# The first packed tile of a two-layer decoder kernel, loaded in two transfers, with one product of zeros fewer ahead of it

## The chip, the cores and the metric

The kernel runs on one core of a Trainium2 chip. The metric is the device time of one execution in microseconds (us); a run is one execution, and the figure for a kernel is the median of its runs. The engines are named as in the profile: PE is the matrix engine (PEld its weight loads), DVE the vector engine, ACT the scalar engine, POOL the general-purpose engine, and SP the engine that issues most of the data transfers (DMAs).

## The reference, cut to what matters

A stack of two layers works on x, 256 tokens of 2048 features, in float32. The first layer is a Mamba-2 mixer, the second a sliding-window attention with a sink per head; each is followed by `layernorm(alpha * x + mixer(x))`.

```python
def reference(x, ...):
    x = layernorm(ALPHA * x + mamba2_mixer(x, a_w_in, ..., a_w_out))
    k, v = shared_kv(x, kv_w, kv_b, cos, sin)
    x = layernorm(ALPHA * x + swa_mixer(x, k, v, cos, sin, b_w_in, ..., b_w_out))
    return x

def mamba2_mixer(x, w_in, ...):
    zxbcdt = x @ w_in                  # z | x,B,C | dt
    dt = softplus(zxbcdt[..., -64:] + dt_bias)     # 64 heads: the step sizes
    ...
```

Only the very first product matters here, `x @ w_in`: its contraction runs over the 2048 features, that is 16 pieces (k = 0 to 15) of 128.

## The kernel before

**Precision.** TensorE is used in a reduced float32 format (fp32r). Every operand v is split into a high part h (a copy on ACT, L158 and L192) and a low part l = v - h (a subtraction on DVE, L161 and L193), and each product is three matmuls, h·h, h·l and l·h (`mac`, L238). The step sizes dt are the exception: they are multiplied in plain float32 (L369).

**Weights.** Weights come as *units* of 128x2048 floats. A unit is loaded in two halves of 512 KB (`load_half`, L149) and split half by half (`split_half`, L158 and L161). Units are loaded two ahead of the one in use (`AHEAD`), in the order of the list `srcs`.

**The start.** The first three units (`NF = 3`, three column blocks of w_in of 128 columns each) do not come as units. The host packs them with x into `first` (L1239): for every k a packed tile of 128 rows by `FW` = 704 floats, which holds 256 columns of x, 128 of each of the three blocks, and the 64 step-size columns at the end. `load_first` (L172) issues the 16 packed tiles one after another on SP's queue (L186), into buffers that are borrowed from other uses (`FIRST`, L33: some lie in the tile that the profile calls xr). For each packed tile it then splits four pieces in this order: x, block 0, block 1, block 2 (ACT at L192, DVE at L193).

`first_products` (L341) writes the order of TensorE's work by hand, with `keep_in_program_order`. First come `FILL[0]` = 6 matmuls of zeros (`fill`, L355), whose result nobody reads; the zeros are set by DVE at L344. Then `_order` (L35) runs over k: at k = 0 the step-size products of packed tile 0 (L369, two of 64x128), then for every k the three blocks' products, three matmuls each (L238, 128x256). Ahead of k = 2 stand `FILL[1]` = 3 more matmuls of zeros. The step-size products of packed tiles 1 to 3 stand ahead of k = 3, those of 4 to 6 ahead of k = 6 and those of 7 to 15 ahead of k = 13. After the 16 k follow the fourth unit and all others, through `block` (L674) and `narrow` (L335), in an order that the kernel plans by block.

**What sets the order.** TensorE's order is the written one. ACT and DVE are ordered by a scheduler that works from estimated times, with a few instructions pinned. SP issues its DMAs in program order. DMAs issued by SP and ACT take eight semaphores in turn, so that a DMA waits until the one eight places before it has landed.

Of the kernel before, what the change touches and what calls it, by code (L numbers as in the profile page):

```python
# [17 lines left out]
P = 128  # L18
S = 256
D = 2048  # L20
KT = D // P
# [3 lines left out]
NHD = 64  # L25
# [6 lines left out]
NF = 3  # L32
FIRST = [("wr", 1)] * 4 + [("yz", 1)] + [("e", 2)] * 2 + [("xr", 5)] + [("rb", 1)] * 2  # L33

def _order():  # L35
    steps = {0: (0, 1), 3: (1, 4), 6: (4, 7), 13: (7, 16)}
    o = []
    for k in range(KT):
        if k in steps:
            o.append((0, *steps[k]))  # L40
        if k == 2:
            o.append(None)
        o += [(i + 1, k, k + 1) for i in range(NF)]
    return o


FILL = [6, 3]

AGAIN = 5
FW = 256 + NF * 128 + 64  # L50

XK_AT = [15, 16, 17, 18]
ZPRI = 200
# [29 lines left out]
def trunk(ctx: ExitStack, tc: tile.TileContext, A: dict, out: bass.AP, dbg=None):  # L83
    nc = tc.nc
# [16 lines left out]
    def nm(s):  # L101
        uid[0] += 1
        return f"{s}_{uid[0]}"

    def mm_tile():
        return mm_ps.tile([P, 512], F32, tag="mm", name=nm("mm"), bufs=4)

    def ax_tile():
        return ax_ps.tile([P, 512], F32, tag="ax", name=nm("ax"), bufs=4)
# [28 lines left out]
    def new_unit(places):  # L138
        u = Unit()
        u.parts = []  # L140
        for tag, n, pl in (("wh", NH, places[0]), ("wl", NL, places[1])):
            t = wp.tile([P, 2112], F32R, tag=tag, name=nm(tag), bufs=n)
            u.parts.append([(t[:, o : o + (k1 - k0) * P], k0, k1) for o, k0, k1 in pl])
        u.h, u.l = u.parts[0][0][0], u.parts[1][0][0]
        return u
# [26 lines left out]
    def load_first():  # L172

        us = [new_unit([WHOLE, WHOLE]) for _ in range(NF)]
        raws = []
        for tag, n in FIRST:
            if tag == "xr":
                buf = xr_t
            elif tag == "wr":
                buf = wp.tile([P, 1024], F32, tag="wr", name=nm("first"), bufs=NR)  # L180
            else:
                w, bufs = {"rb": (1024, 2), "e": (1536, 2), "yz": (1024, 1)}[tag]
                buf = ap.tile([P, w], F32, tag=tag, name=nm("first"), bufs=bufs)
            raws += [buf[:, i * FW : i * FW + FW] for i in range(n)]
        for k, raw in enumerate(raws):
            nc.sync.dma_start(raw, A["first"][:, k, :])  # L186
            parts = [(xH(k, k + 1)[:, 0, :], xL(k, k + 1)[:, 0, :], raw[:, :S])]
            for i, u in enumerate(us):
                ks = slice(k * P, k * P + P)
                parts.append((u.h[:, ks], u.l[:, ks], raw[:, S + i * P : S + i * P + P]))  # L190
            for dh, dl, v in parts:
                nc.scalar.activation(dh, v, AF.Copy)  # L192
                nc.vector.tensor_tensor(dl, v, dh.bitcast(F32), ALU.subtract)  # L193
        return us, raws
# [36 lines left out]
    def next_unit():  # L231
        load_next(min(used[0] + 1 + AHEAD, len(srcs)) - len(units))
        used[0] += 1
        return units[used[0] - 1]
# [100 lines left out]
    def narrow(ps, u, k0, k1, pin=False, again=False):  # L335
        for k in range(k0, k1):
            ks = slice(k * P, (k + 1) * P)
            h, l = [x.again if again and k == 0 else x(k, k + 1)[:, 0, :] for x in (xH, xL)]
            mac(ps[:, :S], u.h[:, ks], u.l[:, ks], h, l, k == 0, k == KT - 1, pin)

    def first_products():  # L341

        zero = ap.tile([P, S], F32, tag="zz", name="zero", bufs=4)
        nc.vector.memset(zero[:], 0.0)  # L344
        zero = zero[:].bitcast(BF16)
        us, raws = load_first()
        units.extend(us)
        nc.sync.dma_start(pc[:], A["pc"])
        pss = [mm_tile() for _ in range(NF + 1)]
        ps = ax_tile()  # L350

        def fill(n):

            for _ in range(n):
                tc.keep_in_program_order(nc.tensor.matmul(ps[:], zero[:, :P], zero, start=True, stop=True))  # L355

        fill(FILL[0])
        for what in _order():
            if what is None:
                fill(FILL[1])  # L360
                continue
            i, k0, k1 = what
            if i:
                narrow(pss[i], us[i - 1], k0, k1, True)
                continue
            for k in range(k0, k1):
                for h in range(2):
                    tc.keep_in_program_order(
                        nc.tensor.matmul(  # L369
                            pss[0][64 * h : 64 * h + 64, :P], raws[k][:, S + NF * P :], raws[k][:, h * P : (h + 1) * P],  # L370
                            start=k == 0, stop=k == KT - 1,
                        )
                    )
        return pss
# [349 lines left out]
    def out_units(g, nbs):  # L724
        for nb in nbs:
            u = next_unit()
            for h in range(2):
                out_unit(*gs[g].y, h, u, nb, False, gs[g].rms)

    first_ps = first_products()  # L730
    dt_first, dt_second = make_dt(first_ps[0])
    load_next(1, True)
# [407 lines left out]
    for what, j in B_ORDER[:-1]:  # L1140
# [5 lines left out]
        else:  # L1146
            for nb in range(4):
                u = next_unit()
# [59 lines left out]
def _layout(inputs):  # L1208
    import numpy as np

    f = {k: np.asarray(v) for k, v in inputs.items()}
    c = np.ascontiguousarray
    a = {}
    x = f["x"][0]
    a["xt"] = c(x.T.reshape(KT, P, S).transpose(1, 0, 2))
    a["xk"] = c(x.reshape(2, P, D).transpose(1, 0, 2))

    def wstat(w):
        k, n = w.shape
        return c(w.reshape(k // P, P, n // P, P).transpose(2, 1, 0, 3).reshape(n // P, P, k))  # L1220

    def xstat(w, per, n):
        k, m = w.shape
        return c(
            w.reshape(k // (per * P), per, P, m // n, n).transpose(3, 0, 2, 1, 4).reshape(-1, P, per * n)
        )

    w = f["a_w_in"][0]
    o_xs, o_b, o_c, o_dt = DI, 2 * DI, 2 * DI + 1024, 2 * DI + 2048
    order = []  # L1230
    for g in range(NG):
        blk = [o_b + g * P, o_c + g * P]
        blk += [o_xs + g * 512 + i * P for i in range(4)]
        blk += [g * 512 + i * P for i in range(4)]
        order += [blk[k] for k in (BLOCKS0 if g == 0 else BLOCKS)]
    cols = np.concatenate([np.arange(s, s + P) for s in order])
    a["wa"] = wstat(w[:, cols])
    wdt = w[:, o_dt:].reshape(KT, P, NHD).transpose(1, 0, 2)
    a["first"] = np.concatenate([a.pop("xt")] + [a["wa"][i].reshape(P, KT, P) for i in range(NF)] + [wdt], 2)  # L1239
    conv = np.concatenate([f["a_conv_w"][0], f["a_conv_b"]], 0)  # L1240
    corder = []
    for g in range(NG):
        corder += [o_b - DI + g * P, o_c - DI + g * P] + [g * 512 + i * P for i in range(4)]
    cv = np.stack([conv[:, s : s + P] for s in corder], 0).transpose(2, 0, 1).reshape(P, 240)
    dsk = np.repeat(f["a_d"][0], 64).reshape(32, P).T
    nw = f["a_norm_w"][0].reshape(32, P).T
    two = lambda v: np.concatenate([v, v])[:, None]
    a["pc"] = c(np.concatenate([cv, dsk, nw, two(f["a_dt_bias"][0]), two(f["a_log"][0])], 1))
    wo = f["a_w_out"][0]
    a["wo"] = xstat(wo, 4, 512).reshape(4, NG, P, 2048).transpose(1, 0, 2, 3).reshape(32, P, 2048)  # L1250
    a["lng"], a["lnb"] = f["ln_g"], f["ln_b"]
    a["gbc"] = c(np.stack([f[k][0].reshape(KT, P).T for k in ("ln_g", "ln_b")], 1))
    a["wkv"] = xstat(f["kv_w"], 4, 512)
    a["kvb"] = f["kv_b"]
    wi = f["b_w_in"][0]
    a["wq"] = xstat(wi[:, :D], 4, 512)
    a["wg"] = wstat(wi[:, D:])
    a["qb"] = f["b_q_bias"][0]
    a["snk"] = f["b_sinks"][0].reshape(4, 4, 2).transpose(0, 2, 1).reshape(32)
    wb = f["b_w_out"][0]  # L1260
    a["wb"] = xstat(wb, 4, 512).reshape(4, 4, P, 2048).transpose(1, 0, 2, 3).reshape(16, P, 2048)
    a["pos"] = c(f["positions"][0].reshape(2, P).T)
    inv = (np.float64(500000.0) ** (-np.arange(0, 16, 2) / 16.0)).astype(np.float32)
    a["inv"] = np.tile(inv[None], (P, 1))
    i = np.arange(P)
    cc = np.zeros((P, 896), np.float32)
    cc[:, 0:128] = np.eye(P)
    cc[:, 128:256] = 1.0
    tri = (i[None, :] >= i[:, None]).astype(np.float32)
    cc[:, 256:384] = tri  # L1270
    cc[:, 384:512] = 1.0
    cc[:, 512:640] = tri
    cc[:, 640:768] = 1.0 - tri
    cc[:, 768:896] = np.where(i[None, :] <= i[:, None], 0.0, NEG)
    a["cc"] = cc
    return {k: c(v) for k, v in a.items()}
# [20 lines left out]
```

## Time and profile before

| | |
|---|---|
| three runs | 1001.87, 1002.36 and 1002.36 us; median 1002.36 |
| the profiled execution: own time | 1002.55 us |
| its span, first to last instruction | 1000.4 us |
| DVE / ACT / POOL busy, of the span | 77% / 57% / 10% |
| DMA | 198.81 MB, on average 199 GB/s |

In the profile's rows the first number is the start in us after the span's start, the second the duration, then engine, source line, operation, output<-inputs, shapes and count. A bracket at the end tells how long the engine was idle before the row and what ended that. "L238" is a line of the kernel before; after the change, lines behind L50 lie two or three further down. Packed tiles appear as `first` or, where the borrowed buffer is that one, as `xr`; `wh` and `wl` are the high and low parts of a unit, `xH` and `xL` those of x.

### The profile page before, as it was taken

To read this page: it belongs to the slowest core of one execution; us is meant where nothing else is said; L and a number is where in the kernel's file an instruction comes from. 1 tells how busy PE (TensorE), PEld (TensorE's weight loads), DVE (VectorE), ACT (ScalarE), POOL (GpSimd) and SP (SyncE) were. 2 spreads that over 40 slices of the span, in tenths; PEclk is the share of its full clock that TensorE was granted. 3 is DMA by queue.
4 is the path that set the end of the run, shared out by engine and by line. 5 is a ranking of instruction groups with operands and counts; after the bars stand their busy time and mean duration, and the time that the engine had idled before them with its cause. 6 is when DMAs were issued, how large, how long until landed. Compare 5 with 4: busy or idle time off the path is not lost.

```text
span 1000.4 us, 17835 instructions
## 1 busy us (share of the span) xinstructions
PE 993.4 (99%) x7036; PEld 899.6 (90%) x7036; DVE 774.6 (77%) x1189; ACT 566.1 (57%) x987; POOL 103.6 (10%) x128
## 2 busy tenths in 40 slices
PE   9999999999999999999999999999999999999997
PEld 8999989999999998999999999888988878878975
DVE  7888897867886886786786787898678775775686
ACT  7595856547746645664654764565545544544632
POOL 0001203004003003000300300303000000000002
PEclk9999999999999999999999999999999999999999
DMA  9798586565575666666656556457764546446422
GB/s 364 249 289 286 169 275 209 174 228 177 181 242 182 223 197 191 212 194 209 206 170 228 159 181 223 164 164 240 240 192 137 193 147 200 156 148 195 166 103 84
DMA packets 58963, 198.81 MB, mean 199 GB/s; under 512 B 6560, under 2 KB 10816, under 8 KB 58624
## 3 DMA queue, kind: packets, MB, share of 16 engines
q1 hardware_dynamic: 55792, 188.20, 57.3%
q0 software_dynamic: 2336, 8.69, 2.8%
q8 instruction: 55, 0.90, 0.4%
q10 hardware_dynamic: 752, 0.79, 0.2%
q14 instruction: 28, 0.23, 0.1%
HBM read 195.43 MB, written 2.23 MB: 198 GB/s over the span
## 4 chain that ended last, share of the span: by engine, by line
PE 95%; DVE 3%; ACT 1%; issue 1%; ACTq 0%; DVEq 0%
PE mm L238 52%; PE mm L945 10%; PE mm L305 8%; PE mm L306 8%; PE mm L307 8%; PE ax L610 2%; PE ax L1057 1%; PE ax L1115 1%; PE ax L586 1%; PE ax L1097 1%; DVE wl L161 1%; PE mm L369 0%; PE ax L569 0%; PE ax L1020 0%; DVE t L1196 0%
## 5 line engine op out<-in xcount | busy, mean ns | idle before, releaser
L161 DVE TENSOR_TENSOR wl<-wr,wh 128x1024 fp32r<-128x1024 f32 (+2 forms) x338 | 393.6, 1185 | 109.1 <-ACT wh L158 107.4
L158 ACT ACTIVATE wh<-wr 128x1024 fp32r<-128x1024 f32 (+2 forms) x338 | 332.7, 1011 | 205.9 <-issue 84.4
L238 PE MATMUL mm<-xH,wh 128*128 128x256 f32 x1280 | 356.1, 278 | 0.0
L238 PE MATMUL mm<-xL,wh 128*128 128x256 f32 x1280 | 354.4, 277 | 0.0
L238 PE MATMUL mm<-xH,wl 128*128 128x256 f32 x1280 | 354.3, 277 | 0.0
L238 PEld LDWEIGHTS mm<-xH,wh 128*128 128x128 f32 x1280 | 240.8, 188 | 2.1 <-ACT wh L192 0.7
L238 PEld LDWEIGHTS mm<-xL,wh 128*128 128x128 f32 x1280 | 240.8, 188 | 1.0
L238 PEld LDWEIGHTS mm<-xH,wl 128*128 128x128 f32 x1280 | 241.0, 188 | 0.0
L305 PE MATMUL mm<-wh,yH 128*128 128x512 f32 x256 | 101.4, 396 | 0.0
L306 PE MATMUL mm<-wh,yL 128*128 128x512 f32 x256 | 99.8, 390 | 0.0
L307 PE MATMUL mm<-wl,yH 128*128 128x512 f32 x256 | 99.7, 389 | 0.0
L626 POOL TENSOR_TENSOR yz<-yz,z 128x256 f32<-128x256 f32 x32 | 32.7, 1032 | 472.7 <-DVE yz L621 472.7
L238 PE MATMUL mm<-x1H,wh 128*128 128x256 f32 x256 | 71.7, 280 | 0.0
L473 DVE SCALAR_TENSOR_TENSOR cv<-mm,pc,cv 128x255 f32<-128x255 f32 x144 | 68.8, 478 | 3.3 <-ACT cv L471 1.9
L238 PE MATMUL mm<-x1L,wh 128*128 128x256 f32 x256 | 70.8, 277 | 0.0
L238 PE MATMUL mm<-x1H,wl 128*128 128x256 f32 x256 | 70.8, 276 | 0.0
L945 PE MATMUL mm<-wh,x1H 128*128 128x512 f32 x160 | 62.9, 393 | 0.0
L945 PE MATMUL mm<-wl,x1H 128*128 128x512 f32 x160 | 62.4, 390 | 0.1
L945 PE MATMUL mm<-wh,x1L 128*128 128x512 f32 x160 | 62.0, 390 | 0.0
L305 PEld LDWEIGHTS mm<-wh,yH 128*128 128x128 f32 x256 | 48.1, 188 | 10.3 <-DVE z L562 1.0
L307 PEld LDWEIGHTS mm<-wl,yH 128*128 128x128 f32 x256 | 48.1, 188 | 10.2
L312 DVE SCALAR_TENSOR_TENSOR xr<-mm,r,xr 128x512 f32<-128x512 f32 x64 | 47.2, 746 | 12.0 <-PE mm L307 7.6
(208 smaller groups left out, 1351.3 us busy)
## 6 DMA issues: line engine op xcount, KB each, us to landing
wr<-in_wa SPq DMA_DIRECT2D x154, 512.0 KB, 5.0
wr<-in_wo SPq DMA_DIRECT2D x64, 512.0 KB, 4.4
wr<-in_wq SPq DMA_DIRECT2D x32, 512.0 KB, 4.6
wr<-in_wg SPq DMA_DIRECT2D x32, 512.0 KB, 4.7
wr<-in_wb SPq DMA_DIRECT2D x32, 512.0 KB, 4.4
rb<-rscr SPq DMA_DIRECT2D x11, 512.0 KB, 4.3
wr<-in_wkv SPq DMA_DIRECT2D x8, 512.0 KB, 5.2
first<-in_first SPq DMA_DIRECT2D x11, 352.0 KB, 6.1
```

What stands on the lines that cost most here:

```text
L158: m = nc.scalar.activation(h[:, sl], v, AF.Copy)
L161: m = nc.vector.tensor_tensor(l[:, sl], v, h[:, sl].bitcast(F32), ALU.subtract)
L238: m = nc.tensor.matmul(ps, a, b, start=first and i == 0, stop=last and i == 2)
L305: pinned(nc.tensor.matmul(ps, aH[:, k, hs], u.h[:, ks], start=k == 0, stop=False), pin)
L306: pinned(nc.tensor.matmul(ps, aL[:, k, hs], u.h[:, ks], start=False, stop=False), pin)
L307: pinned(nc.tensor.matmul(ps, aH[:, k, hs], u.l[:, ks], start=False, stop=k == 3), pin)
L312: nc.vector.scalar_tensor_tensor(v, ps, rms[:, h : h + 1], v, ALU.mult, ALU.add)
L473: nc.vector.scalar_tensor_tensor(a[:, sft:], ps[:, : S - sft], w(3 - sft), a[:, sft:], ALU.mult, ALU.add)
L586: nc.tensor.transpose(ps[:, o : o + P], st.xs[i][:, c * P : (c + 1) * P], ident)
L610: nc.tensor.matmul(ps[64 * r : 64 * r + 64, cols], xd[:, c, r, :], e[:, 256:] if c else e[:, :256], start=c == 0, stop=c == 1,)
L626: nc.gpsimd.tensor_tensor(v, v, st.z[i][:], ALU.mult)
L945: m = nc.tensor.matmul(ps[:], (x1H, x1L, x1H)[i][:, kk, hs], (u.h, u.h, u.l)[i][:, ks], start=(kk, i) == (0, 0), stop=kk == KT - 1 and i == 2,
```

## The change

The packed tile keeps its 704 floats, but the 64 step-size columns now stand behind x and in front of the blocks. Packed tile 0 is loaded in two DMAs, the first of columns 0 to 447 (x, step sizes, block 0), the second of columns 448 to 703 (blocks 1 and 2). The other 15 tiles are loaded whole, as before. `FILL[0]` goes from 6 to 5.

```diff
-FILL = [6, 3]
+FILL = [5, 3]
...
-FW = 256 + NF * 128 + 64
+
+FW = 256 + 64 + NF * 128
+FCUT = 256 + 64 + 128
...
         for k, raw in enumerate(raws):
-            nc.sync.dma_start(raw, A["first"][:, k, :])
+            for c0, c1 in ((0, FCUT), (FCUT, FW)) if k == 0 else ((0, FW),):
+                nc.sync.dma_start(raw[:, c0:c1], A["first"][:, k, c0:c1])
             parts = [(xH(k, k + 1)[:, 0, :], xL(k, k + 1)[:, 0, :], raw[:, :S])]
             for i, u in enumerate(us):
                 ks = slice(k * P, k * P + P)
-                parts.append((u.h[:, ks], u.l[:, ks], raw[:, S + i * P : S + i * P + P]))
+                parts.append((u.h[:, ks], u.l[:, ks], raw[:, S + NHD + i * P : S + NHD + i * P + P]))
...
-                            pss[0][64 * h : 64 * h + 64, :P], raws[k][:, S + NF * P :], raws[k][:, h * P : (h + 1) * P],
+                            pss[0][64 * h : 64 * h + 64, :P], raws[k][:, S : S + NHD], raws[k][:, h * P : (h + 1) * P],
...
-    a["first"] = np.concatenate([a.pop("xt")] + [a["wa"][i].reshape(P, KT, P) for i in range(NF)] + [wdt], 2)
+    a["first"] = np.concatenate([a.pop("xt"), wdt] + [a["wa"][i].reshape(P, KT, P) for i in range(NF)], 2)
```

In the built program TensorE's order is otherwise the same, SP's has one DMA more, and POOL's is unchanged. The scheduler of ACT and DVE puts some instructions in another order: on ACT the evictions of the first three blocks (`in_z`, L561) now stand together, where before the first half of the fifth unit was split between them, and some ten instructions of ACT and DVE change places in the rest of the first group of blocks, before the second unit of the second group.

## The prediction

> **What bounds the kernel now.** I read the page's first lines, then TensorE's waits, then the start of the chain that ended last.
>
> ```profile
> span 1000.4 us, 17835 instructions
> PE 993.4 (99%) x7036; PEld 899.6 (90%) x7036; DVE 774.6 (77%) x1189; ACT 566.1 (57%) x987; POOL 103.6 (10%) x128
> ```
> ```profile
> PE ax L355 <- DVE zero L344: 1.2, 1, 1.2
> PE ax L1182 <- ACT dg L1171: 0.7, 1, 0.7
> ```
> ```profile
> 0.86 0.28 DVE zero L344
> 1.14 0.05 issue
> 1.19 2.74 PE ax L355 x6
> 3.93 0.63 PE mm L369 x4
> 4.56 3.25 PE mm L238 x18
> 7.81 0.66 PE ax L355 x3
> 8.47 1.06 PE mm L238 x9
> ```
>
> TensorE is busy for 993.4 of 1000.4 us, and the waits view lists two waits in the whole run: 1.2 us at the start, until the zeros are written, and 0.7 us in the tail. So there is no wait in between that this change could remove. A change at the start is worth just what it moves TensorE's whole stream forward, and it costs something only if it makes a wait where there is none. The reader is to see in the chain that TensorE goes from six products of zeros straight to the step-size products at 3.93 and the real ones at 4.56. What the change can win lies between 1.19 and 4.56, and one product of zeros is the whole of it.
>
> The rows of those first microseconds:
>
> ```profile
> 2.45 0.15 PEld L355 LDWEIGHTS <-zero 128*128 128x128 bf16 x1 [0.28 <-issue]
> 2.87 0.15 PEld L355 LDWEIGHTS <-zero 128*128 128x128 bf16 x1 [0.28 <-issue]
> ...
> 3.80 0.42 ACT L192 ACTIVATE xH<-first 128x256 fp32r<-128x256 f32 x1 [1.78 <-DMA first<-in_first]
> 3.86 0.30 PEld L369 LDWEIGHTS mm<-first 128*64 128x64 f32 x4 [0.84 <-DMA first<-in_first]
> ...
> 4.49 0.29 PEld L238 LDWEIGHTS mm<-xH,wh 128*128 128x128 f32 x1 [0.33 <-ACT wh L192]
> ```
>
> Zeros follow each other at 0.42 to 0.43 us (2.45 to 2.87). Packed tile 0 releases ACT at 3.80, just as the sixth ends. Two paths meet at the first real product: the zeros' end and the step-size products (3.93 + 0.63 = 4.56), and ACT's start plus 0.69 us for x and block 0 (3.80 to 4.49). Both must move.
>
> **The change, part by part.**
>
> *One product of zeros fewer.* TensorE is free at 3.93 - 0.43 = 3.50. Nothing else hangs on those zeros. This alone would gain nothing, since the data comes at 3.80; it would leave 0.3 us idle.
>
> *A shorter first transfer.* The first piece is 448 of 704 columns, 229 of 360 KB (128 rows of 1792 and 2816 bytes). The trace shows no transfer of this size at an empty queue; this is what it has:
>
> ```profile
> L186 SPq DMA_DIRECT2D first<-in_first x1: 384/384/384, 0.7 to 0.7; - x1
> ...
> DMA to landing us min/median/max: 3.0/3.0/3.0
> ```
> ```profile
> 1.00:2.00 1.00, 0.81 (x2) 0.28 (x3) 0.13 (x1) 1.00 (x1) 0.00 (x0) 1.00 0.28 34
> 2.00:3.00 1.00, 1.00 (x4) 0.43 (x3) 0.00 (x0) 0.01 (x1) 0.00 (x0) 1.00 0.86 276
> 3.00:4.00 1.00, 1.00 (x5) 0.16 (x5) 0.00 (x0) 0.20 (x1) 0.00 (x0) 1.00 1.06 411
> ```
> ```profile
> inv<-in_inv POOLq DMA_DIRECT2D x1, 4.0 KB, 1.9
> ```
>
> The last numbers of the window rows are GB/s: 34 KB have moved by 2.00, 310 by 3.00, and at 411 KB per us the 360 KB of tile 0 are through at 3.12. It lands at 0.74 + 3.0 = 3.74, so 0.62 lie between the last byte and the landing. The first 229 KB are through at 2.00 + 195/276 = 2.71, and land at 3.33: 0.41 us earlier. From the other side, 4 KB take 1.9 us and 360 KB 3.0 us; a straight line through the two gives 0.40 for 131 KB less. Bounds: nothing, if the landing of a first transfer is set by something other than its bytes; and at the other end 0.43, since TensorE isn't free before 3.50. I take 0.41, to which both rows lead.
>
> [...]
>
> *From 0.41 us of start to time at the end.* TensorE is slow here.
>
> ```profile
> 5.75 0.41 PE L238 MATMUL mm<-xH,wl 128*128 128x256 f32 x1
> ...
> 6.18 0.41 PE L238 MATMUL mm<-xL,wh 128*128 128x256 f32 x1
> ...
> 6.39 0.37 PE L238 MATMUL mm<-xH,wl 128*128 128x256 f32 x1
> ...
> 6.60 0.28 PE L238 MATMUL mm<-xH,wh 128*128 128x256 f32 x1
> ...
> 6.72 0.28 PE L238 MATMUL mm<-xL,wh 128*128 128x256 f32 x1
> ```
> ```profile
> 152.20 27.23 PE mm L238 x240
> ```
>
> The granted clock stands at 1.00 in every window row above, but the starts tell of two paces: 0.213 us a product up to 6.39 (three from 5.75) and 0.113 later (27.23/240). The step lies near 6.5 us, 5.3 us after the first product of zeros at 1.19. The zeros still start at 1.19, so I leave the step where it is. TensorE then does 0.41/0.213 = 1.9 products more before the step, and each saves what it would have cost after it: 1.9 x 0.113 = 0.22 us. Half of the gain is lost because it is won at half pace. If the step moved forward with the products, it would be the whole 0.41.
>
> [...]
>
> *The second piece (blocks 1 and 2), a new wait.* ACT's split of block 1 now waits for it, and so does DVE's; behind it in both queues stand block 2 and then packed tile 1, and TensorE's fourth product waits for ACT. ACT comes to it at 3.39 + 0.69 - 0.23 = 3.85 or later. The whole of tile 0 landed at 3.74; the second piece is issued at 0.74 + 0.42, while the engines still work on the first, so it lands about there. Cost: nothing. If it came 0.4 later, block 1's parts would be there at about 4.45, and its first product is due three cold products after 4.15, at 4.8.
>
> *One more DMA on SP.* Its 0.42 us push the issue of tiles 1 to 6 back; tile 7 must now wait for the first piece, which has long landed, and from tile 9 on each waits for the same tile as before. No POOL transfer stands near. How late could tiles 1 and 2 become?
>
> ```profile
> 5.53 0.69 DVE L193 TENSOR_TENSOR wl<-first,wh 128x128 fp32r<-128x128 f32 x3
> ...
> 5.94 0.42 ACT L192 ACTIVATE xH<-first 128x256 fp32r<-128x256 f32 x1 [0.22 <-DMA first<-in_first]
> ...
> 6.73 0.69 DVE L193 TENSOR_TENSOR wl<-first,wh 128x128 fp32r<-128x128 f32 x3
> ...
> 8.12 0.47 PE L238 MATMUL mm<-xH,wh 128*128 128x256 f32 x1
> ```
>
> Tile 1's low parts are done from 5.76 to 6.22; 0.42 later that is 6.18 for the first, which the third product of k = 1 needs at about 6.6. Tile 2's are done by 7.42, 0.70 ahead of the 8.12 at which TensorE comes to k = 2. Take 0.42 of lateness and 0.22 of earlier need away, and 0.06 stays for the last part, which is not needed before the ninth product. So the cost is nothing even at the bound, and the engines' backlog (the DMA share is 0.86 and more from 2.00 on) should hide most of the 0.42 anyway. From there ACT and DVE need under 1 us a tile and TensorE 1.05 and more, so the margin grows.
>
> *Reordered evictions on ACT and DVE.* The order of the two programs differs there.
>
> ```profile
> 26.62 0.38 ACT L561 ACTIVATE z<-mm 128x256 f32<-128x256 f32 x1 [1.48 <-PE mm L238]
> 26.90 1.05 ACT L158 ACTIVATE wh<-wr 128x1024 fp32r<-128x1024 f32 x1
> 27.85 0.65 ACT L561 ACTIVATE z<-mm 128x256 f32<-128x256 f32 x2
> ...
> 28.93 2.35 DVE L161 TENSOR_TENSOR wl<-wr,wh 128x1024 fp32r<-128x1024 f32 x2
> ...
> 66.57 1.22 DVE L161 TENSOR_TENSOR wl<-wr,wh 128x1024 fp32r<-128x1024 f32 x1
> ```
> ```profile
> 23.99 19.69 PE mm L238 x171
> ...
> 61.62 16.35 PE mm L238 x144
> ```
>
> The half unit that stood at 26.90 moves behind the two evictions, by at most 0.65 us. Its unit is the second after the packed ones: TensorE's 171 products from 23.99 begin it after 27 + 48, at 23.99 + 75 x 0.115 = 32.6, while DVE has its low parts at 31.3. 1.3 us of cover against 0.65. Later, one unit's low parts that were ready at 67.8 are due after 96 of the 144 products from 61.62, at 72.5: 4.7 us of cover against moves of one or two instructions of 1.2 to 1.8 us. Cost: nothing.
>
> Sum: -0.22 us. Against the profiled execution's own time 1002.55 that gives 1002.33; the median of the runs lies 0.19 lower, at 1002.36, so the forecast is 1002.14, say 1002.1. A measurement of this kernel tells about 0.2%, 2 us, from no change; this is a tenth of that.
>
> **The rivals.**
>
> *The landing doesn't move* (or only by a tenth). For it: the first transfer takes 3.0 us and 4 KB take 1.9, so most is not bytes. Then TensorE idles from 3.50 to about 3.86 and starts its work where it did: 1002.4, no change. The change does not do what it says.
>
> *The gap sets the pace back: slower.* If the data comes after 3.50, TensorE stands still up to 0.36 us, where the six zeros ran into the data. If standing still makes the count to the fast pace begin anew, the step comes 5.3 us after 3.86, at 9.2 instead of 6.5: 2.7 us more at the slow pace, each of which loses 1 - 0.113/0.213 = 0.47, so +1.27 us: 1003.6. It decides from the point where the first piece lands after 3.50. Against it: 0.36 idle in 5.3 us is 7%. No row here shows how long a stop it takes. [...]
>
> *A unit comes late after the reordering.* A wait of more than 2 us at one of the moved splits would be needed to be seen: 1004.5 and more. Against it stand the covers of 1.3 and 4.7 us.
>
> **How the numbers follow.** The forecast, a gain of 0.1 to 0.43, has 0.60. The landing that does not move has 0.15. The pace set back has 0.12. A late unit or several small losses together over 2 us: 0.10. A gain of more than 2 us, for which I see no place, since TensorE waits 1.9 us in all: 0.03. Faster 0.03, within 0.2% 0.87, slower 0.10. The forecast's own range is 1001.4 (the lowest run, 1001.87, less 0.43) to 1002.6. To leave out no more than 2 in 10 the range takes in the landing that doesn't move and the pace set back: 1001.4 to 1003.6.
>
> **What would show it.** Right: in the chain five zeros end at about 3.50, ACT's first split starts at about 3.4, the first product stands at about 4.15, the step in the pace stays near 6.5, and the first three units end about 0.2 us earlier. Wrong: a bracket of idle time before L369 that names the DMA, a step in the pace later than 7, a wait of ACT at block 1, or any third row in TensorE's waits.

## The result, and the profile after

| | before | after |
|---|---|---|
| median of 21 runs each, in turn on one chip | 1002.12 us (1001.77 to 1003.17) | 1003.15 us (1002.5 to 1006.93) |
| ratio after/before, 95% interval | | 1.0013 [1.0007, 1.0019] |
| profiled execution: own time, span | 1002.55, 1000.4 us | 1004.89, 1002.8 us |

The change made the kernel slower by about 1 us, where 0.22 us of gain was forecast. The profiled execution of after is one of its slower ones (1004.89 against a median of 1003.15); it shows the loss enlarged. The comparisons leave out one run of the experiment merged_fill6 (mean granted clock 0.557, 1671.66 us) and one of before in the same set (0.85, 1101.81 us).

TensorE's waits in after, each row in total us, times, longest:

```profile
PE mm L241 <- ACT wh L195: 1.6, 1, 1.6
PE ax L358 <- DVE zero L347: 1.2, 1, 1.2
PE ax L1185 <- ACT dg L1174: 0.7, 1, 0.7
```

The two waits of before are still there, and the first row is new: TensorE stands 1.6 us for a high part that ACT makes. The start of the chain that ended last (start, duration, what) says what ACT itself had waited for:

```profile
1.65 4.90 DMA first<-in_first
6.58 0.42 ACT xH L195
7.24 2.20 PE mm L241 x9
9.44 1.31 PE ax L358 x3
10.74 1.35 PE mm L241 x9
12.09 0.81 PE mm L372 x12
12.90 3.27 PE mm L241 x27
16.17 0.81 PE mm L372 x12
16.98 7.36 PE mm L241 x63
```

The DMA issued at 1.65 is the third on SP's queue, packed tile 1. It takes 4.90 us and ACT begins to split it at 6.58; in before ACT had begun tile 1 at 4.72. The last row is a good milestone, because the same block of 63 products stands in every variant. In before it is this row:

```profile
14.52 7.36 PE mm L238 x63
```

It begins 2.46 us later in after. From there to the end of the span both need the same: 1002.8 - 16.98 = 985.8 us, and 1000.4 - 14.52 = 985.9. So in these two profiles the whole loss lies in the first 17 us, and the reordered evictions behind them cost nothing.

How the 2.46 come about, from the rows of both chains: in before, 18 products run from 4.56 to 7.81, the first nine of them at 0.213 us, so k = 1 begins at about 6.48; in after at 7.24, 0.76 later. Its nine products take 2.20 in place of 7.81 - 6.48 = 1.33 (0.87 more), the three zeros 1.31 in place of 0.66 (0.65), the next nine 1.35 in place of 1.06 (0.29), and the 27 take 0.10 less. 0.76 + 0.87 + 0.65 + 0.29 - 0.10 = 2.47. A third is the late tile; the rest is slow work behind it. Not all of the 0.87 is the clock: in other profiles nine products behind a wait take 1.53 to 1.55 us at the fast pace. TensorE's products around the wait:

```profile
4.06 0.56 PE L241 MATMUL mm<-xH,wh 128*128 128x256 f32 x1
...
4.75 0.28 PE L241 MATMUL mm<-xH,wh 128*128 128x256 f32 x1
4.87 0.28 PE L241 MATMUL mm<-xL,wh 128*128 128x256 f32 x1
...
7.24 0.38 PE L241 MATMUL mm<-xH,wh 128*128 128x256 f32 x1 [1.63 <-ACT wh L195]
...
7.96 0.42 PE L241 MATMUL mm<-xH,wh 128*128 128x256 f32 x1
8.17 0.41 PE L241 MATMUL mm<-xL,wh 128*128 128x256 f32 x1
```

Tile 0's products start at 4.06, 0.43 earlier than before, as meant, and are at the fast pace (0.12 apart) at 4.75. Behind the wait they are 0.21 apart again. The windows (the last three numbers are granted clock, DMA share and GB/s) show two things:

```profile
3.00:4.00 1.00, 1.00 (x6) 0.30 (x4) 0.16 (x1) 0.61 (x3) 0.00 (x0) 1.00 0.88 109
4.00:5.00 1.00, 1.00 (x8) 0.94 (x7) 0.87 (x4) 0.41 (x3) 0.00 (x0) 1.00 0.73 242
...
7.00:8.00 1.00, 0.76 (x4) 0.67 (x5) 0.98 (x4) 0.86 (x4) 0.00 (x0) 0.94 1.05 414
8.00:9.00 1.00, 1.00 (x6) 1.00 (x6) 0.87 (x5) 1.00 (x6) 0.00 (x0) 0.50 1.05 414
9.00:10.00 1.00, 1.00 (x5) 0.47 (x4) 1.00 (x6) 1.00 (x6) 0.00 (x0) 0.50 1.03 411
10.00:11.00 1.00, 1.00 (x5) 0.80 (x4) 1.00 (x5) 1.00 (x6) 0.00 (x0) 0.50 1.03 411
11.00:12.00 1.00, 1.00 (x8) 0.89 (x7) 1.00 (x6) 1.00 (x6) 0.00 (x0) 0.86 1.03 411
```

First, the engines moved 411 KB between 3 and 4 us before the change and move 109 after it, while tile 1 and its followers stood issued in the queue. Second, the granted clock fell to 0.50 after the wait: a mean of 0.94 in 7 to 8 puts the fall at 7.88, one of 0.86 in 11 to 12 the rise at 11.28. That is 3.40 us.

### The profile page after: what moved, and what is told of

Read it like the earlier page. It is cut to its first block, busy times and chain, and to the rows that moved or that the text cites. A ratio compares the mean times of both kernels' runs of the same rounds, so it can differ in the third digit from the quotient of the medians.

```text
span 1002.8 us, 17839 instructions
## 1 busy us (share of the span) xinstructions
PE 994.0 (99%) x7035; PEld 899.7 (90%) x7035; DVE 774.6 (77%) x1189; ACT 566.0 (56%) x987; POOL 103.6 (10%) x128
## 4 chain that ended last, share of the span: by engine, by line
PE 95%; DVE 3%; ACT 1%; issue 1%; DMA 0%; SPq 0%; ACTq 0%; DVEq 0%
PE mm L241 52%; PE mm L948 10%; PE mm L308 8%; PE mm L309 8%; PE mm L310 8%; PE ax L613 2%; PE ax L1060 1%; PE ax L1118 1%; PE ax L589 1%; PE ax L1100 1%; DVE wl L163 1%; DMA first<-in_first 0%; PE ax L572 0%; PE ax L1023 0%; DVE t L1199 0%
## 5 line engine op out<-in xcount | busy, mean ns | idle before, releaser
L309 PEld LDWEIGHTS mm<-wh,yL 128*128 128x128 f32 x256 | 48.1, 188 | 9.0
```

The source lines that it names most:

```text
L309: pinned(nc.tensor.matmul(ps, aL[:, k, hs], u.h[:, ks], start=False, stop=False), pin)
```

## The experiments

The theories, by the letters that the expectations use. A: a short transfer in second place on SP's queue lets the one behind it, tile 1, come late. B: the profiled execution was a bad one and there is no loss. C: idle time of TensorE in the first microseconds sets the pace back. D: two transfers in place of one, or rows cut in two, cost something by themselves. E and F were added later: E, the third transfer is late whatever the size of the second; F, the loss lies behind the start.

The table gathers the runs. Each ratio is to runs of before in the same set, whose medians are 1002.01 to 1002.18. The fourth column has the tiles 1 to 3 for which ACT waits 0.2 us or more, with the time at which ACT begins them, and the last two columns are of the profiled execution. The start of the 63 products (last but one column) plus 985.7 to 986.1 us is the span in all of them, but for split_fill6, where it is 986.3.

| kernel | zeros | median us, ratio to before | ACT waits for, and begins at | 63 products | span |
|---|---|---|---|---|---|
| before | 6 | 1002.12 | tile 2 5.94, tile 3 7.45 | 14.52 | 1000.4 |
| after | 5 | 1003.15, 1.0013 [1.0007, 1.0019] | tile 1 6.58 | 16.98 | 1002.8 |
| again | 5 | 1003.16, 1.001 [1.0002, 1.0019] | tile 1 5.84, tile 2 8.70 | 15.79 | 1001.6 |
| split_fill6 | 6 | 1003.21, 1.0013 [1.0004, 1.0022] | tile 1 5.67, tile 2 7.08 | 14.59 | 1000.9 |
| split_fill6_b, _c | 6 | 1003.62, 1002.75 (one run each) | tile 1 5.97 and 5.76, tile 2 8.27 and 7.74 | 15.37, 14.84 | 1001.5, 1000.6 |
| whole_fill5 | 5 | 1003.39, 1.0015 [1.0006, 1.0023] | tile 2 6.27, tile 3 8.12 | 15.97 | 1001.7 |
| layout_only | 6 | 1002.11, 1.0 [0.9992, 1.0009] | tile 3 7.43 | 14.61 | 1000.3 |
| split_late | 6 | 1002.17, 1.0 [0.9991, 1.0009] | tile 2 6.86 | 14.54 | 1000.3 |
| pc_second | 6 | 1003.06, 1.001 [1.0001, 1.0019] | tile 1 6.25, tile 2 8.52 | 15.60 | 1001.3 |
| act_piece | 5 | 1003.7, 1.0012 [1.0003, 1.002] | tile 3 7.65 | 15.82 | 1001.6 |
| big_second | 5 | 1002.68, 1.0008 [0.9999, 1.0017] | tile 1 5.71 | 14.64 | 1000.6 |
| keep_pace | 5 + 4 | 1003.05, 1.0012 [1.0002, 1.0021] | tile 1 6.01 | 14.96 | 1000.9 |
| fill10 | 10 | 1002.99, 1.0009 [1.0, 1.0018] | tile 2 6.34, tile 3 8.07 | 14.64 | 1000.3 |
| merged | 5 | 1002.65, 1.0005 [0.9996, 1.0014] | tile 3 7.97 | 13.91 | 999.7 |
| merged_fill6 | 6 | 1001.65, 0.9998 [0.9988, 1.0007] | | | |
| merged_fill6_b | 6 | 1001.85, 0.9995 [0.9986, 1.0004] | tile 2 7.42 | 14.51 | 1000.2 |

**again**: the changed kernel once more, no edit.

> The changed kernel once more, for a second profile. In its first profile packed tile 1 landed at 6.55 us (4.9 us after its issue) instead of about 4.6, TensorE waited 1.6 us for it, and the pace fell back to half from 7.5 to 11.2. Theory A (a short second transfer lets the transfer engines run dry, and they start up anew): tile 1 lands at 6.0 to 6.8 again, the wait is there again, and the time is 0.4 to 2 us above the kernel before, depending on where the slow pace falls. Theory B (a single bad execution): tile 1 lands at 4.6 to 5.1, no wait, and the time is within 0.3 us of before.

The same median again, so B falls. ACT begins tile 1 at 5.84, a little sooner than A had it. The profile shows two shorter waits in place of one, no fall of the clock, and tile 2 as the one that counts:

```profile
PE mm L241 <- ACT wh L195: 1.5, 2, 0.8
```
```profile
2.12 6.56 DMA first<-in_first
...
15.79 7.36 PE mm L241 x63
```

**split_fill6**, and its two repeats: the split, with the old number of zeros.

```diff
-FILL = [5, 3]
+FILL = [6, 3]
```

> The changed kernel with six products of zeros as before, so the two transfers alone. Theory A: tile 1 lands at 6.0 to 6.8, TensorE waits 1 to 1.6 us for it, and the time is that of the changed kernel, 0.5 to 2 us above before. Theory C (the missing product of zeros makes TensorE's start idle and sets the pace back; the transfers do no harm): no wait, 0 to 0.3 us below before.

> The changed kernel with six products of zeros, once more, one look at where its typical 1003.2 us arises. Theory A+C: tile 1 lands at 5.6 to 6.5 us and is waited for, or the pace is lost, in most executions: the block of 63 products begins at 15 us or later, and the span is that start plus 985.8 us. Rival F (the loss lies behind the start, in GpSimd's chain of squares at 109 us, from the moved evictions): the block begins at 14.6 us as in the first look, TensorE waits for GpSimd at 109 us, and the span is the start plus 986.3 us or more.

> The same once more. Theory A+C: the block of 63 products begins at 15 us or later, the span is that start plus 985.8 us. Rival F: the block begins at 14.6 us, TensorE waits for GpSimd at 109 us, and the span is the start plus 986.3 us or more.

As slow as the change, so the split alone is enough; the missing zeros are not needed for the loss. In the first profile the pace was slow until about 5.7 us, tile 0's products so lasted until tile 1 was there, and only GpSimd's chain was late: the wait of 1 to 1.6 us that A named is not in this profile. In the repeats (rows of split_fill6, then of split_fill6_b and of split_fill6_c) that wait is gone and the wait for tile 1 is there:

```profile
PE ax L653 <- POOL sq L635: 0.3, 1, 0.3
```
```profile
PE mm L241 <- ACT wh L195: 0.6, 1, 0.6
...
15.37 7.36 PE mm L241 x63
```
```profile
PE mm L241 <- ACT wh L195: 0.6, 1, 0.6
...
14.84 7.36 PE mm L241 x63
```

F is not what sets the median. A's number (15 or later) came in one repeat, and 14.84 in the other.

**whole_fill5**: the new layout of the tile, loaded whole, with five zeros.

```diff
-            for c0, c1 in ((0, FCUT), (FCUT, FW)) if k == 0 else ((0, FW),):
+            for c0, c1 in ((0, FW),):
```

> The changed layout with tile 0 in one transfer and five products of zeros, so the missing product alone. Theory A: tile 1 lands at 4.6 as before; TensorE is idle 0.3 us ahead of the first real product, and the time is within 0.3 us of before. Theory C: the step to the fast pace comes later than 7 us, and the time is 0.5 to 1.5 us above before.

Here tile 0 comes after the zeros end, and TensorE stands 0.6 us:

```profile
PE mm L372 <- DMA first<-in_first: 0.6, 1, 0.6
```
```profile
4.77 4.21 PE mm L241 x18
8.99 1.04 PE ax L358 x3
...
15.97 7.36 PE mm L241 x63
```

18 products in 4.21 us where before took 3.25, and zeros still slow at 9: the pace was set back. This is the prediction's second rival in its own condition. Priced there at +1.27, it measures 1003.39 - 1002.11 = +1.28 in the medians, with an interval of 0.6 to 2.3 us. That the two agree so closely is in part luck: the wait was 0.6 us and not 0.36, and the fast pace comes only among the three zeros, between 9 and 10 us, where the rival had 9.2. So C happens, for a kernel whose tile 0 comes too late. In the changed kernel tile 0 does not.

**layout_only** (whole_fill5 with `FILL = [6, 3]`) and **split_late** (the same, with packed tile 4 in two pieces in place of none).

```diff
-            for c0, c1 in ((0, FW),):
+            for c0, c1 in ((0, FCUT), (FCUT, FW)) if k == 4 else ((0, FW),):
```

> The changed layout of the packed tile, loaded whole, with six products of zeros: neither of the two edits that were found to cost about 1.1 to 1.3 us. If those two edits are the whole of it, this is the kernel before: within 0.3 us of it, tile 1 landing at 4.5 to 4.9, no wait of TensorE. If the layout itself costs something (the step sizes now lie between x and the blocks), it is 0.5 us or more above before.

> As layout_only, but packed tile 4 comes in two transfers (448 and 256 columns) instead of tile 0: the same two short transfers and one DMA more, at a place where the transfer engines have a backlog and TensorE has its data a microsecond ahead. If the loss of the split is in the place (the second and third transfer of a queue that has just started), this is within 0.4 us of before and tile 1 lands at 4.5 to 4.9. If it is in the extra DMA or the short rows anywhere, tile 5 lands 1 to 2 us late and the time is 0.5 us or more above before.

Both take what before takes. The new layout costs nothing, and a tile in two pieces costs nothing as the fifth tile: D falls as a general price. It is the place that matters.

**pc_second**: before, with the load of the constants `pc` (153 KB) issued right behind tile 0, and no tile cut.

```diff
             nc.sync.dma_start(raw, A["first"][:, k, :])
+            if k == 0:
+                nc.sync.dma_start(pc[:], A["pc"])
...
-        nc.sync.dma_start(pc[:], A["pc"])
```

> The kernel before, with its 153 KB transfer of constants (pc) issued right behind packed tile 0 instead of after the last one; nothing is split, six products of zeros. Theory A in its narrow form (any short transfer in second place lets the engines run dry): tile 1 lands 1.5 us or more later than its share of bytes explains, at 6 or later, and the time is 0.5 us or more above before. Theory D (it is the two short pieces one after the other, or the cut rows, that do it): tile 1 lands 0.4 us later, at about 5.0, for 153 KB at 400 KB per us, and the time is within 0.3 us of before.

As slow as the change, with neither a cut tile nor a missing product of zeros. The third DMA of the queue, now tile 1 issued at 1.65, reaches ACT at 6.25, and the fourth takes 6.38 us:

```profile
6.25 0.42 ACT L194 ACTIVATE xH<-first 128x256 fp32r<-128x256 f32 x1 [1.31 <-DMA first<-in_first]
```
```profile
2.12 6.38 DMA first<-in_first
...
15.60 7.35 PE mm L240 x63
```

**act_piece** (the second piece issued by ACT, on its own queue) and **big_second** (the cut at 320 columns: 164 KB, then 197 KB).

```diff
-                nc.sync.dma_start(raw[:, c0:c1], A["first"][:, k, c0:c1])
+                (nc.scalar if c0 else nc.sync).dma_start(raw[:, c0:c1], A["first"][:, k, c0:c1])
```
```diff
-FCUT = 256 + 64 + 128
+FCUT = 256 + 64
```

> The changed kernel with the second piece of tile 0 issued by ACT instead of SP; five products of zeros. SP's queue is then first piece, tile 1, tile 2 and so on. If the stall comes from what stands second in SP's queue, tile 1 lands at 4.3 to 4.9, TensorE has no wait, and the time is 0.1 to 0.3 us below before (the gain that was forecast). If the engines stall on the third transfer whatever queue issues it, tile 1 lands at 5.6 or later and the time is 0.5 to 1.5 us above before.

> The changed kernel with the cut at 320 columns in place of 448: x and the step sizes first (164 KB), then all three blocks (197 KB). Theory A, by size (it is the shortness of the second transfer that lets the engines run dry): 197 KB against 131 shortens the stall, tile 1 lands at about 5.3 to 5.8 us in place of 5.8 to 6.6, and the kernel takes some 1002.6 us. Rival E (the third transfer of the queue stalls for about a microsecond, whatever the second's size, so long as the first two hold one tile): tile 1 lands at 5.8 to 6.6 us as in the changed kernel, 1003.1 us.

In act_piece the short second transfer is gone from SP's queue, and tile 1 is on time (4.79):

```profile
3.82 0.42 ACT L195 ACTIVATE xH<-first 128x256 fp32r<-128x256 f32 x1 [1.36 <-DMA first<-in_first]
...
4.79 0.42 ACT L195 ACTIVATE xH<-first 128x256 fp32r<-128x256 f32 x1
```
```profile
PE mm L372 <- DMA first<-in_first: 0.3, 1, 0.3
```
```profile
4.54 4.21 PE mm L241 x18
```

But the two pieces, issued side by side at 0.73 and 0.74, take 3.1 and 3.2 us to land, where the first takes 2.6 in after. It reaches ACT at 3.82 and not at 3.39, and five zeros end before it. In this profile 0.3 us of standing goes with the same 4.21 us for 18 products as in whole_fill5, where it is 0.6. One loss was exchanged for the other, and the gain that was expected for a tile 1 on time did not come.

In big_second the dip is milder, and tile 1 comes at 5.71:

```profile
3.00:4.00 1.00, 1.00 (x6) 0.30 (x4) 0.43 (x1) 0.73 (x3) 0.00 (x0) 1.00 1.02 222
```

The median 1002.68 is A's number (1002.6) and not E's (1003.1), but the interval holds both.

**keep_pace** (the change, with four products of zeros between tile 0's products and tile 1's) and **fill10** (before, with ten zeros at the start).

```diff
-FILL = [5, 3]
+FILL = [5, 3, 4]
...
-        if k == 2:
+        if k in (1, 2):
             o.append(None)
...
```
```diff
-FILL = [6, 3]
+FILL = [10, 3]
```

> The changed kernel with four products of zeros more, between tile 0's products and tile 1's. Tile 1's landing is not touched. Theory C (of the loss, a part is the late tile itself, and a part the slow pace after TensorE's idle time): the zeros fill some 0.9 us of the wait of 0.8 to 1.6 us, the pace is kept, and what is left is the late tile alone: 1002.2 to 1002.7 us, and a smaller spread than the changed kernel's. Rival (the loss is the late tile alone, idle or not): 1003.1 us, as the changed kernel, or more by zeros that run past tile 1's landing.

> The kernel before with ten products of zeros ahead of tile 0 in place of six; tile 0 has then landed for about 1.9 us when TensorE comes to it. The prediction's step 3 (time won or lost at the slow pace counts by 1 less 0.113/0.213, about half): four zeros of 0.43 us, some 1.7 us later at the slow pace, cost 0.9 us: 1003.0 us. Rival (a late start is paid in full): 1003.8 us. Rival (the start is hidden behind the landings of tiles 2 and 3 anyway): 1002.1 us.

keep_pace missed C's number and came out at its rival's. In its profile the pace was slow to begin with, tile 0's products lasted until 6.34, and the zeros then ran for 0.88 us more, to 7.22. Tile 1 had reached ACT at 6.01, and its first high part is there 0.66 us after that (6.58 to 7.24 in after), so at 6.67: the zeros held TensorE 0.55 us past it.

```profile
6.34 0.88 PE ax L358 x4
```

Zeros at a fixed place are themselves a delay when the pace is slow, so the run does not separate the late tile from the lost pace.

In fill10 four zeros cost 1002.99 - 1002.01 = 0.98 us in the medians, against 0.9 by half price and 1.7 in full; the interval of 0 to 1.8 excludes neither of the rivals. Its profile tells more:

```profile
1.19 4.06 PE ax L355 x10
...
14.64 7.36 PE mm L238 x63
```

Ten zeros in 4.06 us are, as an estimate, nine at 0.43 and one at 0.22, so the step to the fast pace lay near 5.0 us here. By step 3's rule four more zeros at the fast pace cost 0.88 us, and a step 1.5 us earlier than in before gives 1.5 x 0.47 = 0.70 back. That makes 0.18, and the 63 products begin 14.64 - 14.52 = 0.12 later. So the rule holds in this profile, and a single execution can hide the cost.

**merged**, **merged_fill6** and **merged_fill6_b**: the first piece grows to 576 columns (295 KB), and block 2 travels with tile 1 in one transfer of 426 KB. Tiles 0 and 1 lie side by side in one buffer for that.

```diff
-FCUT = 256 + 64 + 128
+FCUT = 256 + 64 + 256
...
-            for c0, c1 in ((0, FCUT), (FCUT, FW)) if k == 0 else ((0, FW),):
-                nc.sync.dma_start(raw[:, c0:c1], A["first"][:, k, c0:c1])
+            if k == 0:
+                nc.sync.dma_start(raw[:, :FCUT], A["first"][:, 0, :FCUT])
+                nc.sync.dma_start(two[:, FCUT:], A["first"].rearrange("p k f -> p (k f)")[:, FCUT : 2 * FW])
+            elif k > 1:
+                nc.sync.dma_start(raw, A["first"][:, k, :])
```

> A first transfer of x, step sizes and two blocks (576 columns, 295 KB), then one transfer of the last block together with the whole of tile 1 (832 columns, 426 KB), then the rest: as many DMAs as before and none short behind another; five products of zeros. The first two tiles lie in a borrowed buffer of two tiles for this, so the buffers of the others change places. If a short second transfer is what stalls the engines, tile 1 lands at 4.5 to 5.0 and the time is within 0.4 us of before, on either side. If any transfer shorter than a tile at the head does it, tile 1 lands at 5.6 or later and the time is 0.5 us or more above before.

> As the kernel with the short second piece merged into tile 1's transfer, but with six products of zeros again. [...] Rival D (two transfers where one was, or rows cut in two, cost something by themselves): 1002.6 or more, as with five zeros.

> The kernel with the second piece merged into tile 1's transfer and six products of zeros, once more, for a profile of an execution at the full clock and a second set of times. Theory A+C (no short second transfer, no gap): TensorE waits for no tile at the start, tile 1 lands by 5.2 us, the block of 63 products begins at 14.2 to 15.0 us, and the median is 1001.7 to 1002.2. Rival D (two transfers where one was cost something by themselves): 1002.6 or more.

Here tile 0 is cut in two and no second transfer is short. With six zeros the loss is gone: 1001.65 and 1001.85, and D's 1002.6 came in neither. With five zeros the median is 1002.65, 0.47 us above before and a little more than the 0.4 expected. TensorE waits 0.2 us for the first piece in the profile; that execution kept its pace and is the fastest profiled (span 999.7), but the runs spread from 1001.44 to 1003.78, against 1001.28 to 1002.26 in merged_fill6_b. Rows of merged, then of merged_fill6_b:

```profile
PE mm L377 <- DMA first<-in_first: 0.2, 1, 0.2
...
13.91 7.35 PE mm L246 x63
```
```profile
7.42 0.42 ACT L200 ACTIVATE xH<-first 128x256 fp32r<-128x256 f32 x1 [1.51 <-DMA first<-in_first]
...
14.51 7.35 PE mm L246 x63
```

In merged_fill6_b, too, the third transfer (tile 2) was late, at 7.42. Two tiles were already there, TensorE waited 0.2 us, and the block of 63 began as in before. No version beats before by more than its interval.

**The third DMA in all profiles.** In every variant the third DMA of SP's queue is a whole tile of 360 KB, issued at 1.65. From issue to landing it takes, in the sixteen profiles of the table above:

| in second place on SP's queue | third DMA, us |
|---|---|
| 131 to 197 KB | after 4.9, again 4.2, split_fill6 4.0, _b 4.3, _c 4.1, pc_second 4.6, big_second 4.0, keep_pace 4.3 |
| 360 or 426 KB | before 4.3, whole_fill5 4.6, layout_only 3.9, split_late 5.2, act_piece 4.1, fill10 4.7, merged 4.2, merged_fill6_b 5.8 |

Two of these rows, of split_fill6 and of merged_fill6_b:

```profile
DMA to landing us min/median/max: 4.0/4.0/4.0
```
```profile
DMA to landing us min/median/max: 5.8/5.8/5.8
```

In these profiles a short DMA in second place does not make the third one later, so A has the mechanism wrong. What the cut did was to push tile 1 from the second place into the third. The second DMA takes 3.4 to 3.7 us where it is a tile or more. ACT begins tile 1 at 4.72 to 5.12 us in the eight profiles where it stands second on SP's queue, and at 5.67 to 6.58 in the eight where it stands third. This is nearer to E, though the 5.71 of big_second lies in A's range.

## Why the prediction was wrong, point by point

- **One product of zeros fewer, a shorter first transfer: right.** ACT began x of tile 0 at 3.39 (forecast about 3.4, before 3.80), and the products at 4.06, 0.43 earlier. The first piece is steady: ACT begins it at 3.36 to 3.42 in six profiles. The whole first tile is not: 3.80 to 4.07 in six, and before's 3.80 is the earliest. So the rival that the landing doesn't move falls, and that the 0.41 came out so exactly is in part luck.
- **From start to end: the rule was right, the step's place was not.** fill10's profile agrees with half price. But the step to the fast pace was left at 6.5 us as if it were fixed. It came before 4.75 in after, near 4.9 in split_fill6_b, near 5.7 in split_fill6 and near 6.9 in layout_only, all with the zeros beginning at 1.19. One us of step is 0.47 us of time, so the step's place alone moves a run by more than the 0.22 us that was forecast.
- **The second piece, a new wait: right.** TensorE's nine products of tile 0 run on without a wait for blocks 1 and 2.
- **One more DMA on SP: this step failed.** It said that tile 1 can be at most 0.42 us late, because the issue is 0.42 later, that "the cost is nothing even at the bound", and that the backlog of the engines hides most of it. The issue was the least of it: the step took landing to follow issue, and by the runs it goes by the place in the queue. Tile 1's DMA took 4.90 us from issue to landing, where in before it took 3.4 in second place and the DMA in third place 4.3 (its tile 2); the engines moved 109 KB in the microsecond in which they had moved 411. By before's own third place tile 1 would land at 1.65 + 4.3 = 5.95. The rows of before, for its DMAs issued at 1.18 and at 1.65:

```profile
DMA to landing us min/median/max: 3.4/3.4/3.4
```
```profile
DMA to landing us min/median/max: 4.3/4.3/4.3
```

  ACT began tile 1 at 6.58, 5.84, 5.67, 5.97 and 5.76 us in the five profiles of the split with that cut and no added zeros between, against 4.72: 0.95 to 1.86 us later. Four of the five are within 0.3 us of that 5.95, and after is 0.63 above it. This part of the prediction also took only 0.22 us off tile 1's cover, since it held the change of pace to be fixed. In after tile 0's products end at 7.24 - 1.63 = 5.61 and not near 6.5, which lays bare more of the same lateness. The prediction's last sign, a third row in TensorE's waits, came true. pc_second shows the step's failure without the rest of the change, and merged_fill6 a cut tile 0 without the failure.
- **Reordered evictions: right within 0.5 us.** The time from the 63 products to the end is 985.8 us in after, against before's 985.9. One of three profiles of split_fill6 shows 0.3 us for GpSimd's squares.
- **The rival "gap sets the pace back": price right, place wrong.** It was to decide when the first piece lands after 3.50; the piece landed in time. Where that condition was made true (whole_fill5, act_piece) its price came. In after the clock did fall, but behind the wait for tile 1, which no rival had. In again the same wait, cut into two of at most 0.8 us, did not bring it down. That 1003.15 is inside the stated range is luck: the range reaches so high for this rival, and the loss has another cause.

What stays open is why the third DMA takes so long, and why the throughput dips. In every profile here the third or the fourth transfer of SP's queue makes ACT wait, and the throughput has its lowest microsecond around it, between 3 and 6 us (109 GB/s in after, 293 in before, 338 in pc_second); before has it too. Between 3 and 4 us the engines move 109 to 222 KB in the seven profiles with tile 0 cut ahead of a third-place tile 1, and 377 to 420 KB in the nine others. That 360 KB are through before the third DMA begins to move would fit this, but no run tests it. What is shown is what it costs: with two tiles landed ahead of the dip nothing can be measured, with one about 1 us.

## What to carry to other kernels

Cutting the first transfer of a queue to start earlier doesn't only delay the ones behind it by an issue slot: it moves each of them one place back (here ACT began tile 1 at 5.67 to 6.58 us from the third place, against 4.72 to 5.12 from the second). Read from the kernel before how long each of the first four transfers takes from issue to landing, and give a tile the landing of its new place; then ask how much data has landed by then. Where an engine starts at a slow pace, as TensorE here (0.213 us a product, then 0.113), a wait in the first microseconds can cost more than its length (in whole_fill5 one of 0.6 us went with 1.28 us in the medians), and an earlier start is worth less than its length: by these two paces 0.113/0.213 = 0.53 of it, as an estimate. A gain of a fifth of a microsecond at the start is below what the start itself varies by: the first whole tile reached ACT at 3.80 to 4.07 us in six profiles.

## What the runs showed of the hardware

- The third DMA of SP's queue, a tile of 360 KB, took 3.9 to 5.8 us from issue to landing in sixteen profiles, whether 131 or 426 KB stood ahead of it in second place; before's first took 3.0 and its second 3.4. The fourth took 6.56 us in again and 6.38 in pc_second, against 5.3 in before.
- Behind a wait of 1.6 us after fast products the granted clock stood at 0.50 for 3.40 us (after). A wait of 0.6 us at the start went with a longer slow pace (whole_fill5: the zeros ahead of k = 2 take 0.35 us each at 9 us, against 0.22 in before), and one of 0.2 us did not (split_late, merged: 0.22 each). At the start the clock's record reads 1.00 at the slow pace too (before, 5 to 6 us: 1.00, with products 0.213 us apart).
- The nine products behind a wait for a tile take 1.53 to 1.55 us at the fast pace in place of 1.06, presumably since ACT's and DVE's splits of that tile then run just ahead of them; that was not tried.
